# Gate projections as seven quarter products in a stage of their own, their sigmoids kept in DRAM

## The chip, the cores and the metric

The kernel runs on one core of a Trainium2 chip. The metric is the device time of one execution in microseconds (us). Before the change it is 2252.72 us, the median of three runs (2252.09 to 2253.51).

## What is computed

The reference is one decoder layer over 1024 tokens of width 1024, in float32. Three branches y_a (a linear recurrence), y_b (sliding-window attention) and y_c (dilated attention) read the same x. Each has a gate, and they are merged:

```python
proj = x @ w_in                      # gates: 3 x 1024 of its columns
...
ys = jnp.stack([y_a, y_b, y_c], axis=2)
branch = jnp.einsum('bsnc,ncd->bsnd', ys, w_branch)
merged = jnp.sum(jax.nn.sigmoid(gates.reshape(bsz, S, N_BRANCHES, D)) * branch, axis=2)
return merged @ w_out
```

A layer norm, a SwiGLU feed-forward part of width 2816 and a second layer norm follow.

## The kernel before

Activations lie transposed, channels on the 128 partitions and tokens along the free axis. Every float32 matrix product is made of three float32r products: an operand is split into `hi` (a cast on ScalarE, ACT) and `lo` (a subtraction on VectorE, DVE), and hi*hi, hi*lo and lo*hi are added in PSUM. So one 128-column chunk of a weight (8 k tiles of 128 x 128) against one half of the tokens (512) is 24 matmuls of 128x512.

The stages in order of time: projections and recurrence of branch a (to about 190 us), attention of y_b (to 440), attention of y_c (to 944), the gate and branch stage (944 to 1466), the output projection with the first layer norm (to 1599), the first feed-forward product (to 2002), the second with the last norm.

`WeightStream` (lines 44 to 126) feeds the weights. Each source is a chunk of 512 KB, loaded on SP's queue into a ring of two `w_raw` tiles, then split into `w_hi` and `w_lo` (rings of two). A step of the stream is a generator that issues matmuls and yields.

The gate and branch stage (lines 775 to 850 and 902 to 911) is a list `seq` of 48 jobs: three gate jobs, then a branch job and a gate job in turn. A gate job multiplies one chunk of the gate columns of `w_in` with `xh`/`xl`, the split x that has stayed in SBUF since the start; `gate_evac` writes the sigmoid into a ring of three `sg` tiles. A branch job does the same with a chunk of `w_branch` and with `yh`/`yl`, the split output of one branch, which `load_y` reads back from DRAM (`y_dram`). `branch_evac` multiplies by the sigmoid and adds to `merged`.

The first feed-forward product (lines 1054 to 1200) is done by seven products of quarters, Winograd's form of Strassen's scheme. The operand x is cut into four quarters, two halves of k by two halves of the tokens, and so are two weight chunks of 128 columns. Seven products (`a00`, `a01`, `s1` to `s4`, `a11`) of 12 matmuls each, 84 in a pair, stand for the eight (96 matmuls) of the plain way. POOL makes four sums `t` of weight quarters per pair, ACT and DVE split five half chunks (`ph`, `pl`) and, in all but the first four pairs, one whole chunk; DVE adds the banks in SBUF tiles `e`. In the first four pairs ("front" pairs) the products `a00` and `a01` have been done earlier, since their x quarters are ready first.

The order of instructions on each engine is not the order of the code alone: the scheduler of the framework reorders what has no dependence between it.

Of the kernel before, what the change touches and what calls it, by code (L numbers as in the profile page):

```python
# [148 lines left out]
def trunk_kernel(ctx: ExitStack, tc: tile.TileContext, x, x_t, w_in, conv_w, conv_b, w_rg, b_rg, w_ig, b_ig,  # L149
# [17 lines left out]
    x1_dram = dram.tile([KT, P, D], F32, name="x1_dram")  # L167
    g_dram = dram.tile([2, HT, P, HALF], F32, name="g_dram")
# [592 lines left out]

    drain(W.run(lead))
# [8 lines left out]
    va.close()  # L771
# [3 lines left out]
    a3 = ExitStack()  # L775
    acc8 = mk_pool(ctx, "acc8", bufs=8, space=PSUM)
    mg1 = mk_pool(a3, "mg1")
    mg3 = mk_pool(a3, "mg3", bufs=3)
    mg4 = mk_pool(a3, "mg4", bufs=4)
    merged = mg1.tile([P, KT, S], F32, name="merged")  # L780
    order = (1, 2, 0)
    LEAD = 3
    NB = 3 * KT
    sg = {}
    yparts = {}

    def load_y(n, hf):
        yh = mg1.tile([P, KT, HALF], F32R, tag=f"yh{hf}", name="yh")
        yl = mg1.tile([P, KT, HALF], F32R, tag=f"yl{hf}", name="yl")
        for k in range(KT):  # L790
            t = mg4.tile([P, HALF], F32, tag="yraw", name="yraw")
            act.dma_start(t, y_dram[n][k, :, hf * HALF:(hf + 1) * HALF])
            act.copy(yh[:, k, :], t)
            dve.tensor_sub(yl[:, k, :], t, yh[:, k, :].bitcast(F32))
        yparts[n, hf] = yh, yl

    def gate_evac(i):
        def f(hf, acc):
            if hf == 0:
                sg[i] = mg3.tile([P, S], F32, tag="sg", name="sg")  # L800
            act.activation(sg[i][:, hf * HALF:(hf + 1) * HALF], acc, AF.Sigmoid)
        return f
# [3 lines left out]
    def branch_evac(i):  # L806
        bi, dt = divmod(i, KT)

        def f(hf, acc):
            sl = slice(hf * HALF, (hf + 1) * HALF)  # L810
            m = merged[:, dt, sl]
            if bi == 0:
                dve.tensor_mul(m, sg[i][:, sl], acc)
                return
            t = sg[i][:, sl]
            dve.tensor_mul(t, t, acc)
            dve.tensor_add(m, m, t)
            first = NB - LEAD
            if i >= first:
                if i == first:  # L820
                    fin_h[hf] = xpool.tile([P, KT, HALF], F32R, tag=f"xh{hf}", name="mh")
                    fin_l[hf] = xpool.tile([P, KT, HALF], F32R, tag=f"xl{hf}", name="ml")
                for d in range(0 if i == first else dt, dt + 1):
                    m = merged[:, d, sl]
                    act.copy(fin_h[hf][:, d, :], m)
                    dve.tensor_sub(fin_l[hf][:, d, :], m, fin_h[hf][:, d, :].bitcast(F32))
        return f

    def gate_job(i):
        bi, dt = divmod(i, KT)  # L830
        proj_job(acc8, w_cols(w_in, C_G + order[bi] * D + dt * P), x_mov, gate_evac(i))

    def branch_job(i):
        bi, dt = divmod(i, KT)
        n = order[bi]

        def movs(hf, k):
            yh, yl = yparts[n, hf]
            return yh[:, k, :], yl[:, k, :]
        proj_job(acc8, w_cols(w_branch[n], dt * P), movs, branch_evac(i))  # L840

    seq = [("g", i) for i in range(LEAD)]
    for i in range(NB):
        seq.append(("b", i))
        if i + LEAD < NB:
            seq.append(("g", i + LEAD))
    ends = []
    for kind, i in seq:
        (gate_job if kind == "g" else branch_job)(i)
        ends.append(len(W.steps))  # L850
# [50 lines left out]

    load_y(order[0], 0)
    load_y(order[0], 1)
    for (kind, i), end in zip(seq, ends):
        last_of_branch = kind == "b" and i % KT == KT - 1 and i // KT < 2
        for j, c in enumerate(W.run(end)):
            if last_of_branch and j == 4:
                load_y(order[i // KT + 1], 0)
        if last_of_branch:
            load_y(order[i // KT + 1], 1)  # L910
    a3.close()

# [67 lines left out]

# [73 lines left out]
    def product(bank, op, bh, bl, start):  # L1054

        ah, al = ops[op]
        for k in range(4):
            wh, wl = bh[:, k * P:(k + 1) * P], bl[:, k * P:(k + 1) * P]
            mm(bank, wh, ah[:, k, :], start and k == 0, False)
            mm(bank, wh, al[:, k, :], False, False)  # L1060
            mm(bank, wl, ah[:, k, :], False, k == 3)
            if k % 2:
                yield 1296

    NA = 4
    front = {}

    def front_evac(bank, q):

        if q == 0:  # L1070
            t = frp.tile([P, HALF], F32, tag="p1", bufs=NA, name="p1")
            act.copy(t, bank)
        else:
            t = frp.tile([P, HALF], F32, tag="silu", bufs=NA, name="silu")
            act.activation(t, bank, AF.Silu)
        return t

    def front_step(j):

        def f(hi, lo):  # L1080
            bank = acc8.tile([P, HALF], F32, tag="acc", name="acc")
            got = []
            for q in range(2):
                sl = slice(q * HALF, (q + 1) * HALF)
                yield from product(bank, L_OPS[q], hi[:, sl], lo[:, sl], q == 0)
                got.append(front_evac(bank, q))
            front[j] = got
        W.add([w_cols(w_ffn_in, j * P)], [(0, f)])

    for j in range(NA):  # L1090
        front_step(j)
# [9 lines left out]
    sring = mk_pool(srS, "sring", side="right")  # L1101
    raws, parts = {}, {}

    def load_pair(j):
        raws[j] = []
        for c in (j * P, FF + j * P):
            t = stage.tile([P, 1024], F32, tag="w_raw", name="w_raw")
            sync.dma_start(t.rearrange("p (a b) -> p a b", b=P), w_cols(w_ffn_in, c))
            raws[j].append(t)

    def wsum(j, n, a, b, op):
        t = sring.tile([P, HALF], F32, tag="t", bufs=3, name="t")
        pool.tensor_tensor(t, a, b, op=op)  # L1113
        raws[j, n] = t

    def wsplit(j, n, src, width=HALF):
        if width == HALF:
            hi = sring.tile([P, HALF], F32R, tag="ph", bufs=7, name="ph")
            lo = sring.tile([P, HALF], F32R, tag="pl", bufs=7, name="pl")
        else:  # L1120
            hi = stage.tile([P, 1024], F32R, tag="w_hi", name="w_hi")
            lo = stage.tile([P, 1024], F32R, tag="w_lo", name="w_lo")
        act.copy(hi, src)  # L1123
        dve.tensor_sub(lo, src, hi.bitcast(F32))  # L1124
        parts[j, n] = hi, lo

    def prep(j):


        def b(k, c):  # L1130
            return raws[j][c][:, k * HALF:(k + 1) * HALF]

        def p1():
            wsum(j, "t1", b(0, 1), b(0, 0), OP.subtract)
            wsum(j, "t2", b(1, 1), raws[j, "t1"], OP.subtract)

        def p2():
            if j not in front:
                wsplit(j, "b0", raws[j][0], D)

        def p5():
            wsum(j, "t3", b(1, 1), b(0, 1), OP.subtract)
            wsplit(j, "t3", raws[j, "t3"])

        def p6():
            wsplit(j, "b11", b(1, 1))
            wsum(j, "t4", b(1, 0), raws[j, "t2"], OP.subtract)
            wsplit(j, "t4", raws[j, "t4"])
        return [lambda: load_pair(j), p1, p2, lambda: wsplit(j, "t2", raws[j, "t2"]),
                lambda: wsplit(j, "t1", raws[j, "t1"]), p5, p6]  # L1150

    def temp():
        return sring.tile([P, HALF], F32, tag="e", bufs=6, name="e")
# [3 lines left out]

    def pair(j, between):


        if j in front:
            between(0)
            p1, silu = front.pop(j)
        else:
            b0h, b0l = parts.pop((j, "b0"))
            ba = bank_()
            between(0)
            yield from product(ba, "a00", b0h[:, :HALF], b0l[:, :HALF], True)
            p1 = front_evac(ba, 0)
        between(1)  # L1170
        bb = bank_()
        yield from product(bb, "s2", *parts.pop((j, "t2")), True)
        u2 = temp()
        dve.tensor_add(u2, p1, bb)
        between(2)
        bc = bank_()
        yield from product(bc, "s1", *parts.pop((j, "t1")), True)
        v = temp()
        dve.tensor_add(v, u2, bc)
        between(3)  # L1180
        bd = bank_()
        yield from product(bd, "s3", *parts.pop((j, "t3")), True)
        dve.tensor_add(v, v, bd)
        between(4)
# [156 lines left out]
```

## Time and profile before

| | |
|---|---|
| profiled execution | 2260.57 us, of which 2258.8 us span |
| median of the three timed runs | 2252.72 us |
| TensorE (PE) busy | 98% of the span |
| VectorE (DVE), ScalarE (ACT), GpSimd (POOL) busy | 59%, 41%, 19% |
| granted TensorE clock, mean | 0.992 |
| DMA, mean over the span | 89 GB/s |

The span is from the first to the last instruction. A busy PE is not a PE at its peak: matmuls overlap, and each is shown longer than the distance to the next one. What a stretch costs is read from the starts: a row of the chain of waits that says "us, PE ..., xN" gives the distance of matmuls as us divided by N.

### The profile page before, as it was taken

The page shows a single profiled execution, that of the slowest core. Times are in us where ns is not written, and L with a number is a line of the kernel's source. Part 1 is how long each engine was busy: PE and PEld are TensorE (multiplying, and loading weights), DVE is VectorE, ACT ScalarE, POOL GpSimd, SP SyncE. Part 2 cuts the span into 40 slices and gives each one's busy share as a digit, 9 for nine tenths or more (in the row PEclk, how much of TensorE's full clock was granted, in tenths as well). Part 3 has the DMA queues.
Part 4 walks back from the last instruction along what each step waited for, and adds up shares of the span by engine and source line. Part 5 has one row for each costly group of instructions (what it writes and reads, how often), then busy time and mean ns, then how long its engine had stood idle before and what let it go on. Part 6 is the DMA issues. An engine that isn't in the chain of part 4 may idle for free.

```text
span 2258.8 us, 29437 instructions
## 1 busy us (share of the span) xinstructions
PE 2205.9 (98%) x11161; PEld 1870.4 (83%) x11161; DVE 1341.0 (59%) x2554; ACT 924.2 (41%) x1748; POOL 440.1 (19%) x411
## 2 busy tenths in 40 slices
PE   8999999999999999999999999999899999999998
PEld 6787888988899888888888888888778888888786
DVE  7888888776867768721142242459665445453735
ACT  4765776655655655521131131223233333342321
POOL 2332222212221222100000000002344334400301
PEclk9999999999999999999999999999999999999999
DMA  5123123112222223331131131154232222254543
GB/s 150 47 80 96 47 66 78 49 48 64 49 57 55 57 68 107 113 98 47 47 121 51 52 103 47 47 166 151 79 108 84 84 84 84 82 194 149 184 154 114
DMA packets 200654, 201.19 MB, mean 89 GB/s; under 512 B 9600, under 2 KB 156096, under 8 KB 200512
## 3 DMA queue, kind: packets, MB, share of 16 engines
q1 hardware_dynamic: 171232, 126.89, 18.7%
q0 software_dynamic: 14880, 45.14, 7.0%
q10 hardware_dynamic: 14400, 27.27, 3.8%
q8 instruction: 88, 1.44, 0.3%
q14 instruction: 54, 0.44, 0.1%
HBM read 152.08 MB, written 36.70 MB: 84 GB/s over the span
## 4 chain that ended last, share of the span: by engine, by line
PE 83%; DVE 9%; DMA 3%; issue 2%; ACT 2%; POOL 1%; SPq 0%; DVEq 0%; POOLq 0%; ACTq 0%
PE acc L185 71%; PE o L185 4%; PE s L185 4%; PE pt L542 4%; DVE xc L385 1%; DVE w_lo L97 1%; DMA w_raw<-in_w_ffn_in_dram 1%; DMA xin<-in_x_t_dram 1%; DVE pl L1124 1%; DMA x_dram<-r 1%; DVE r L964 1%; DVE r L961 1%; DMA res<-in_x_dram 1%; POOL t L1113 0%; DVE xc L382 0%
## 5 line engine op out<-in xcount | busy, mean ns | idle before, releaser
L185 PE MATMUL acc<-xh,w_hi 128*128 128x512 f32 x1056 | 418.7, 397 | 13.0 <-ACT w_hi L96 7.1
L185 PE MATMUL acc<-xl,w_hi 128*128 128x512 f32 x1056 | 415.8, 394 | 0.0
L185 PE MATMUL acc<-xh,w_lo 128*128 128x512 f32 x1056 | 415.4, 393 | 0.0
L96 ACT CAST w_hi<-w_raw 128x1024 fp32r<-128x1024 f32 x149 | 156.7, 1052 | 432.5 <-PE acc L185 390.1
L97 DVE TENSOR_TENSOR w_lo<-w_raw,w_hi 128x1024 fp32r<-128x1024 f32 x111 | 140.7, 1268 | 288.1 <-ACT w_hi L96 288.0
L185 PEld LDWEIGHTS acc<-xh,w_hi 128*128 128x128 f32 x1056 | 199.5, 189 | 52.4 <-ACT w_hi L96 7.1
L185 PEld LDWEIGHTS acc<-xh,w_lo 128*128 128x128 f32 x1056 | 199.4, 189 | 39.7 <-DVE w_lo L97 0.8
L185 PEld LDWEIGHTS acc<-xl,w_hi 128*128 128x128 f32 x1056 | 199.7, 189 | 37.4
L965 POOL TENSOR_TENSOR r<-r,ln_b 128x1024 f32<-128x1024 f32 x13 | 38.6, 2976 | 695.7 <-DMA res<-in_x_dram 572.8
L546 ACT CAST pt_h<-pt 128x512 fp32r<-128x512 f32 (+3 forms) x256 | 124.8, 500 | 92.3 <-PE pt L542 87.5
L547 DVE TENSOR_TENSOR pt_l<-pt,pt_h 128x512 fp32r<-128x512 f32 (+3 forms) x256 | 144.3, 572 | 20.7 <-ACT pt_h L546 18.3
L185 PE MATMUL acc<-yh,w_hi 128*128 128x512 f32 x384 | 149.4, 389 | 0.0
L185 PE MATMUL acc<-yl,w_hi 128*128 128x512 f32 x384 | 149.4, 389 | 0.0
L185 PE MATMUL acc<-yh,w_lo 128*128 128x512 f32 x384 | 149.4, 389 | 0.0
L537 POOL DMA_DIRECT2D y_dram<-yp x96 | 52.1, 543 | 425.2 <-DVE yp L536 326.2
L542 PE MATMUL pt<-ident,p 128*128 128x128 f32 x816 | 129.9, 278 | 1.6 <-DVE pt_l L547 0.8
L185 PE MATMUL o<-pt_h,v 128*128 128x256 f32 (+1 forms) x464 | 117.4, 275 | 1.8 <-DVE yp L536 1.8
L1123 ACT CAST ph<-t 128x512 fp32r<-128x512 f32 x88 | 53.9, 622 | 154.8 <-PE acc L185 82.1
L185 PE MATMUL acc<-w_lo,gh 128*128 128x512 f32 x288 | 113.2, 393 | 4.0 <-DVE w_lo L97 4.0
L185 PE MATMUL o<-pt_l,v 128*128 128x256 f32 (+1 forms) x464 | 113.9, 286 | 2.1 <-DVE pt_l L547 2.1
L629 ACT ACTIVATE p<-p,small 128x128 f32<-128x128 f32 (+7 forms) x128 | 99.5, 778 | 37.4 <-DVE small L626 36.0
L185 PE MATMUL acc<-w_hi,gl 128*128 128x512 f32 x288 | 112.9, 392 | 0.0
(330 smaller groups left out, 5071.9 us busy)
## 6 DMA issues: line engine op xcount, KB each, us to landing
w_raw<-in_w_in_dram SPq DMA_DIRECT2D x76, 512.0 KB, 3.8
w_raw<-in_w_ffn_in_dram SPq DMA_DIRECT2D x48, 512.0 KB, 4.5
w_raw<-in_w_ffn_out_dram SPq DMA_DIRECT2D x47, 512.0 KB, 3.7
w_raw<-in_w_branch_dram SPq DMA_DIRECT2D x24, 512.0 KB, 3.9
yraw<-y_dram ACTq DMA_DIRECT2D x48, 256.0 KB, 3.4
g_dram<-e POOLq DMA_DIRECT2D x44, 256.0 KB, 3.0
w_raw<-in_w_out_dram SPq DMA_DIRECT2D x12, 512.0 KB, 3.7
gl<-g_dram SPq DMA_DIRECT2D x22, 256.0 KB, 4.2
```

The source lines that it names most:

```text
L96: self.nc.scalar.copy(hi, raw)
L97: self.lo_engine.tensor_sub(lo, raw, hi.bitcast(F32))
L185: pe.matmul(o, a, b, start=start, stop=stop, skip_group_check=True)
L385: dve.scalar_tensor_tensor(xc, xr[:, 1 + j:1 + j + S], vec[:, j * 8 + ct:j * 8 + ct + 1], xc, op0=OP.mult, op1=OP.add)
L537: pool.dma_start(dst, yp[:, :n])
L542: pe.transpose(pt[:, i * P:(i + 1) * P], b, ident)
L546: act.copy(dst_h, v)
L547: dve.tensor_sub(dst_l, v, dst_h.bitcast(F32))
L629: act.activation(p[:, :n], p[:, :n], AF.Exp, bias=m, scale=-1.0, accum_out=sm[:, 1:2])
L961: dve.tensor_scalar(r[:, sl], r[:, sl], mv[:, 0:1], sm[:, 3:4], op0=OP.subtract, op1=OP.mult)
L965: adder.tensor_add(r[:, sl], r[:, sl], lnp["b"][:, sl])
L1123: act.copy(hi, src)
```

## The change

The sigmoids of all gates are computed in a stage ahead of the branch products, by the seven-product scheme, and written to a new DRAM buffer `sg_dram`; the branch stage reads them back, one 512 KB tile for each job. The code of the feed-forward pairs becomes a class `Pairs` that both stages use. For the feed-forward part its order differs in this: the last step of a pair's preparation (`b11` and `t4`) is made in the pair itself instead of in the one before, the next pair's load is issued two products later, `t4` is made in place of `t2` (two `t` tiles instead of three), and one sum is made in place of `u2`.

The x quarters for the sums are loaded again from the transposed input `x_t` (`load_xq`), two of the four k tiles on SP's queue in the last part of the attention and two on ACT's queue behind it; POOL and DVE make the sums (`x_sums`), ACT and DVE split them (`x_split`).

```diff
+    def load_xq(k, where, queue):
+        t = where.tile([P, 4, HALF], F32, tag="v", name="xq")
+        for q in range(4):
+            r, c = (q % 2 * 4 + k) * P, q // 2 * HALF
+            queue.dma_start(t[:, q, :], x_t[r:r + P, c:c + HALF])
+        xq[k] = [t[:, q, :] for q in range(4)]
+    def x_sums(k, eng):
+        a00, a01, a10, a11 = xq[k]
+        eng.tensor_add(a11, a10, a11)
+        eng.tensor_sub(a10, a00, a10)
+        eng.tensor_sub(a00, a11, a00)
+        pool.tensor_sub(a01, a01, a00)
...
+        if units is todo[-1][0]:
+            for k in range(2):
+                load_xq(k, vpool, sync)
+            for k in range(2):
+                x_sums(k, pool)
...
+        def pair(self, j, between):
...
+            between(1)
+            bb = self.bank()
+            yield from product(bb, "s2", *parts.pop((j, "t2")), True)
+            u2 = temp()
+            dve.tensor_add(u2, p1, bb)
+            between(2)
+            bc = self.bank()
+            yield from product(bc, "s1", *parts.pop((j, "t1")), True)
+            v = temp()
+            dve.tensor_add(v, u2, bc)
+            between(3)
+            bd = self.bank()
+            yield from product(bd, "s3", *parts.pop((j, "t3")), True)
+            dve.tensor_add(v, v, bd)
+            self.c11(j, v)
+            between(4)
+            if j >= self.na:
+                yield from product(ba, "a01", b0h[:, HALF:], b0l[:, HALF:], False)
+                self.c00(j, ba)
+            between(5)
+            yield from product(bc, "s4", *parts.pop((j, "b11")), False)
...
+            between(6)
+            yield from product(bd, "a11", *parts.pop((j, "t4")), False)
+            dve.tensor_add(u2, u2, bd)
+            self.c10(j, u2)
...
+                def between(i):
+                    if i == 1:
+                        cur[6]()
+                    elif nxt:
+                        for f in {2: nxt[:1], 4: nxt[1:3], 5: nxt[3:4], 6: nxt[4:6]}.get(i, ()):
+                            f()
...
+    NG = 3
...
+    def sig_out(j, tile_, half_, src, dst):
+        act.activation(dst, src, AF.Sigmoid)
+        act.dma_start(sg_dram[2 * j + tile_, :, half_ * HALF:(half_ + 1) * HALF], dst)
...
+    def x_split(k):
+        a00, a01, a10, a11 = xq[k]
+        for n, src in (("s2", a00), ("s1", a11), ("s3", a10), ("s4", a01)):
+            h, l = [o[:, k, :] for o in xops[n]]
+            act.copy(h, src)
+            dve.tensor_sub(l, src, h.bitcast(F32))
+    load_xq(2, vpool, act)
+    load_xq(3, yx, act)
+    for j in range(NG):
+        gate.front_step(j, j == 2)
...
+    def load_sg(i):
+        if i < NB:
+            sg[i] = mg3.tile([P, S], F32, tag="sg", name="sg")
+            pool.dma_start(sg[i], sg_dram[i])
-    def gate_job(i):
-        bi, dt = divmod(i, KT)
-        proj_job(acc8, w_cols(w_in, C_G + order[bi] * D + dt * P), x_mov, gate_evac(i))
...
+    gate.run(12, at, first, 2)
...
+    load_y(order[0], 1)
+    for n_, end in enumerate(ends):
+        for _ in W.run(end):
+            pass
+        if n_ % 7 == 1 and n_ < 14:
+            load_y(order[n_ // 7 + 1], 0)
+        if n_ == 2:
+            load_y(order[1], 1)
+        if n_ == 13:
+            load_y(order[2], 1)
```

Before, PE goes from the third gate chunk (`xh`, `xl` with `w_hi`, `w_lo`) to the first branch chunk (`yh`, `yl`), and on in turn:

```order
L185 MATMUL acc<-xh_93,w_hi 128x512
L185 MATMUL acc<-xl_95,w_hi 128x512
L185 MATMUL acc<-xh_93,w_lo 128x512
L185 MATMUL acc<-yh,w_hi 128x512
L185 MATMUL acc<-yl,w_hi 128x512
L185 MATMUL acc<-yh,w_lo 128x512
```

Now PE goes from the last front product (x quarter `xh_93` with half-chunk splits `ph`, `pl`) to the first pair's products, which read the split sums `gs2` (and `s1`, in the place of `xh_94`):

```order
L186 MATMUL acc<-xh_93,pl 128x512
L186 MATMUL acc<-gs2h,ph 128x512
L186 MATMUL acc<-gs2l,ph 128x512
L186 MATMUL acc<-xh_94,ph 128x512
L186 MATMUL acc<-xl_96,ph 128x512
L186 MATMUL acc<-gs2h,pl 128x512
```

72 front matmuls stand where the 144 of the three gate chunks stood first, and the pair's products come ahead of all branch work.

On DVE, the same place before: behind the last attention output (`yp`) come the `lo` parts of the first y (`yl`) and of the weights:

```order
L536 TENSOR_TENSOR yp<-o,yp 64x256
L794 TENSOR_TENSOR yl<-yraw,yh 128x512 x8
L97 TENSOR_TENSOR w_lo<-w_raw,w_hi 128x1024
L794 TENSOR_TENSOR yl<-yraw,yh 128x512 x8
L97 TENSOR_TENSOR w_lo<-w_raw,w_hi 128x1024 x2
```

And now, at the same place (the end of this stretch; `xq` are sums of x quarters, `gs2l` to `gs4l` and `xl_96` splits of them, `yv` the first y, `pl` splits of weight sums, `e` the first sum out of PSUM):

```order
L778 TENSOR_TENSOR xq<-xq 128x512
L1031 TENSOR_TENSOR yv<-yv 128x512 x2
L875 TENSOR_TENSOR pl<-t,ph 128x512 x2
L1031 TENSOR_TENSOR yv<-yv 128x512
L992 TENSOR_TENSOR gs3l<-xq,gs3h 128x512
L1031 TENSOR_TENSOR yv<-yv 128x512
L992 TENSOR_TENSOR gs2l<-xq,gs2h 128x512
L992 TENSOR_TENSOR gs4l<-xq,gs4h 128x512
L875 TENSOR_TENSOR pl<-t,ph 128x512
L875 TENSOR_TENSOR pl<-w_raw,ph 128x512
L875 TENSOR_TENSOR pl<-t,ph 128x512
L923 TENSOR_TENSOR e<-p_10225,acc 128x512
```

Between `yp` and that first `e` there are 31 DVE instructions of 128x512 now: 6 sums, 14 splits of sums, 4 of y, 2 of the third front chunk and 5 of the first pair's weights.

At the end of the gate stage, ACT issues the loads of the second half of the first y (`y_dram_58`) and of both halves of the second (`y_dram_59`) in one piece, mixed with the last sigmoids:

```order
L1029 DMA yl<-y_dram_58 128x512
L96 CAST w_hi<-w_raw 128x1024
L979 DMA sg_dram<-e 128x512
L1030 CAST yh<-yl 128x512
L1029 DMA yl<-y_dram_59 128x512
L1030 CAST yh<-yl 128x512
L1029 DMA yl<-y_dram_59 128x512
L978 ACTIVATE e<-e 128x512
```

Before, those loads were spread over two changes of branch.

## Rows read from the trace of the kernel before

**Rows 1.** Page, part 1: PE's busy time, share of the span, instructions.

```profile
PE 2205.9 (98%) x11161; PEld 1870.4 (83%) x11161; DVE 1341.0 (59%) x2554; ACT 924.2 (41%) x1748; POOL 440.1 (19%) x411
```

**Rows 2.** Windows: stretch and us; engines' busy us (count); PEclk, DMA share, GB/s.

```profile
944.20:1466.50 522.30, 522.30 (x2305) 432.60 (x2305) 150.67 (x189) 113.69 (x161) 0.53 (x1) 1.00 0.24 72
1560.00:1598.80 38.80, 33.52 (x174) 28.53 (x172) 33.27 (x48) 19.18 (x35) 4.53 (x3) 0.91 0.28 89
1598.80:1656.90 58.10, 55.27 (x230) 43.42 (x230) 37.08 (x49) 15.91 (x27) 26.37 (x23) 0.97 0.32 98
1656.90:2004.00 347.10, 347.10 (x1531) 287.53 (x1532) 178.23 (x246) 109.32 (x169) 129.26 (x106) 1.00 0.29 93
```

**Rows 3.** Chain of waits, whole span: start us, us, what was waited for.

```profile
944.20 561.55 PE acc L185 x2477
...
1656.89 454.32 PE acc L185 x2003
```

**Rows 4.** Groups by line, gate and branch stage: busy us, mean ns, idle before.

```profile
L185 PE MATMUL acc<-xh,w_hi 128*128 128x512 f32 x384 | 149.4, 389 | 0.0
...
L794 DVE TENSOR_TENSOR yl<-yraw,yh 128x512 fp32r<-128x512 f32 x48 | 31.9, 689 | 26.3 <-ACT yh L793 26.1
L793 ACT CAST yh<-yraw 128x512 fp32r<-128x512 f32 x48 | 28.9, 620 | 34.9 <-DMA yraw<-y_dram 19.9 <-PE acc L185 8.2 <-issue 4.1
L801 ACT ACTIVATE sg<-acc 128x512 f32<-128x512 f32 x48 | 28.4, 592 | 90.4 <-PE acc L185 88.0 <-DVE yl L794 1.9 <-issue 0.5
```

**Rows 5.** Groups by line, full pairs of the feed-forward stage.

```profile
L1124 DVE TENSOR_TENSOR pl<-t,ph 128x512 fp32r<-128x512 f32 x69 | 55.5, 804 | 15.7 <-ACT ph L1123 15.7
...
L1113 POOL TENSOR_TENSOR t<-w_raw 128x512 f32<-128x512 f32 x34 | 44.1, 1297 | 149.3 <-DMA w_raw<-in_w_ffn_in_dram 149.3
...
L1124 DVE TENSOR_TENSOR w_lo<-w_raw,w_hi 128x1024 fp32r<-128x1024 f32 x17 | 22.6, 1329 | 39.1 <-ACT w_hi L1123 39.1
...
L1179 DVE TENSOR_TENSOR e<-e,acc 128x512 f32<-128x512 f32 x18 | 12.4, 686 | 20.7 <-PE acc L185 20.7
```

**Rows 6.** Timeline of ACT from 944 us: start, us, instruction, idle before.

```profile
944.24 4.37 ACTq L792 DMA_DIRECT2D yraw<-y_dram  x4
948.71 0.62 ACT L793 CAST yh<-yraw 128x512 fp32r<-128x512 f32 x1 [4.11 <-issue]
950.07 0.62 ACT L793 CAST yh<-yraw 128x512 fp32r<-128x512 f32 x1 [0.74 <-DMA yraw<-y_dram]
950.13 0.33 ACTq L792 DMA_DIRECT2D yraw<-y_dram  x1
950.98 0.62 ACT L793 CAST yh<-yraw 128x512 fp32r<-128x512 f32 x1 [0.28 <-DMA yraw<-y_dram]
```

**Rows 7.** Timeline around 1614 us, POOL and DVE side by side.

```profile
1614.02 1.62 POOL L1113 TENSOR_TENSOR t<-w_raw,t 128x512 f32<-128x512 f32 x1 [1.29 <-DVE pl L1124]
1614.40 1.78 DVE L1124 TENSOR_TENSOR pl<-w_raw,ph 128x512 fp32r<-128x512 f32 x1
```

**Rows 8.** Waits of PE, 1560 to 2004 us: total us, times, longest.

```profile
PE acc L185 <- ACT ph L1123: 2.5, 3, 1.6
PE acc L185 <- DVE e L1179: 1.8, 2, 1.1
```

**Rows 9.** Chain of waits through the front pairs of the feed-forward stage.

```profile
1603.39 5.26 DMA w_raw<-in_w_ffn_in_dram
...
1608.82 1.30 POOL t L1113
...
1610.18 1.30 POOL t L1113
...
1612.16 1.28 DVE pl L1124 x2
...
1616.72 4.78 DMA w_raw<-in_w_ffn_in_dram
```

**Rows 10.** DMA issues: count, KB each, median us to landing.

```profile
yraw<-y_dram ACTq DMA_DIRECT2D x48, 256.0 KB, 3.4
```

More of the change, by code (lines that the diff above doesn't have):

```diff
@@ new lines, in trunk_kernel @@
+    load_xq(2, vpool, act)
+    load_xq(3, yx, act)
+    for j in range(NG):
+        gate.front_step(j, j == 2)
+    first = gate.prep(0)
+    for i, _ in enumerate(W.run()):
+        if i == 0:
+            gate.own_front(2)
+        if i % 2 == 0 and 2 <= i <= 8:
+            k = i // 2 - 1
+            if k >= 2:
+                x_sums(k, dve)
+            x_split(k)
+        if i == 8:
+            first[0]()
+            first[1]()
+    place = {(1, 0): 0, (1, 1): 1, (2, 0): 2, (2, 1): 3, (0, 0): 0, (0, 1): 3}
@@ L783, in trunk_kernel @@
     NB = 3 * KT
+    AHEAD = 3
+    yq = []
     sg = {}
@@ L900, in trunk_kernel @@
                             [wo_dest(k) for k in range(n)]))
[L902 to L910, printed above, removed]
     a3.close()
+    va.close()
     ff1 = mk_pool(ctx, "ff1")
@@ L1052, in trunk_kernel, with ffn_c00, ffn_c11, ffn_c01 @@
     later.extend(op_transposes((0, 1)))
[L1054 to L1063, printed above, removed]
-    NA = 4
[L1066 to L1088, printed above, removed]
+    NA = 4
+    silu = {}
+    sringp = []
+    def ffn_c00(j, bank):
+        t = frp.tile([P, HALF], F32, tag="silu", bufs=NA, name="silu")
+        act.activation(t, bank, AF.Silu)
+        silu[j] = t
+    def ffn_c11(j, v):
+        silu[j, 1] = v
+    def ffn_c01(j, g):
+        dve.tensor_mul(g, g, silu.pop(j))
+        pool.dma_start(g_dram[0, j], g)
+    def ffn_c10(j, g):
+        act.activation(g, g, AF.Silu)
+        dve.tensor_mul(g, g, silu.pop((j, 1)))
+        pool.dma_start(g_dram[1, j], g)
+    ffn = Pairs(lambda j: [w_cols(w_ffn_in, c) for c in (j * P, FF + j * P)], ops, sringp, [frp], NA,
+                ffn_c00, ffn_c01, ffn_c10, ffn_c11)
     for j in range(NA):
-        front_step(j)
+        ffn.front_step(j)
     run_steps(W.run(), 2)
@@ L1100, in trunk_kernel @@
     srS = ExitStack()
[L1101 to L1150, printed above, removed]
@@ L1152, in temp @@
[L1152 to L1153 removed]
+    sringp.append(mk_pool(srS, "sring", side="right"))
     def bank_():
         return acc8.tile([P, HALF], F32, tag="acc", name="acc")
[L1158 to L1184, printed above, removed]
[L1185 to L1200 removed]
@@ L1280, in ffn_done @@
             later.extend(rest)
-    for f in prep(0):
-        f()
-    for j in range(HT):
-        nxt = prep(j + 1) if j + 1 < HT else []
-        drain(pair(j, lambda n: nxt[n]() if nxt else None))
+    ffn.run(HT)
     srS.close()
```

228 lines of the change are left out of this document (170 added, 58 removed).

## The prediction

> **What bounds the kernel now.** I read part 1 of the page first: PE is busy for 98% of the span, and no other engine reaches 60% [rows 1]. That is an average, so the second view is the windows by stage. In the gate and branch stage PE is busy for all of 522.30 us at the full granted clock, while DVE, ACT and POOL work 150.67, 113.69 and 0.53 us [rows 2]. The groups of this stage say the same from the other side: PE waited 0.0 us before its matmuls, and ACT's sigmoids spent 88.0 us waiting for PE [rows 4]. Third, the chain of waits gives the price of a matmul. From 944.20 it is one piece, 561.55 us for 2477 matmuls, 0.2267 us each; the feed-forward part gives 454.32/2003 = 0.2268 us [rows 3]. So this stage is matmuls end to end, and its time is their number times 0.2268 us, as long as the other engines keep ahead. Fourth, the feed-forward stage shows what the new scheme does here. Its full pairs, 1656.9 to 2004, have PE busy for 347.10 of 347.10 us, but its beginning does not: 55.27 of 58.10 us in the front pairs and 33.52 of 38.80 us just before, with clocks of 0.97 and 0.91 [rows 2].
>
> **Removed: matmuls.** Before, 24 gate chunks of 48 matmuls (24 for each half of the tokens) are 1152. Now 12 pairs of 84 are 1008. 144 x 0.2268 = -32.7 us. The branch products keep their 1152. All of it lies on the bounding engine, so it counts in full.
>
> **Added: the start of the gate stage, +4.5 us.** PE's first work is the front products, 72 matmuls whose x quarters have stayed split in SBUF; then s2 and s1 of the first pair (12 each). s2 needs a split sum of all four k tiles, s3 another. From 944.2 PE has 96 x 0.2268 = 21.8 us of work if s2 is in time, so s3 is wanted at 966.0. Two of the four k tiles come only by loads that ACT issues behind the attention. Four such loads stand at this very place before: issued from 944.24, their casts start at 948.71 to 950.98 [rows 6], so I let the x quarters of k = 2 be there at 950.5. Behind them DVE has a fixed list, shown under the change: 29 instructions of 128x512 up to the lo part of t3's split. At 0.689 us [rows 4] that is 20.0 us, which ends at 970.5, 4.5 us late. ACT has fewer (its casts take 0.62 us [rows 6]) and does not set the end. What stands behind DVE's list in its queue are the evacuations, with 8 PSUM banks as slack.
>
> **The same start with POOL beside DVE: +2.** POOL makes two x sums and t1, t2, t3, t4 of the first pair in this stretch, 6 x 1.297 us [rows 5] = 7.8 us. One row pair shows the two engines side by side: a POOL sum took 1.62 us and a DVE split, begun during it, 1.78 us in place of 0.69 [rows 7], so 1.1 us was lost in that meeting. Over many, the mean is lighter: DVE's pl takes 0.804 us in the full pairs, where POOL's sums run too, against 0.689 without them [rows 4, 5]; 69 x 0.115 = 7.9 us, over 17 pairs of four sums 0.12 us a sum. So 6 sums cost between 0.7 and 7.8 us. I take 2, nearer the mean than the single meeting, since DVE's list is dense here and so meets more.
> The Trainium skill, "SBUF — State Buffer", section "SBUF: two separate sides", calls the pair of ports that DVE and GpSimd share an exclusive lock: the loser blocks for the whole instruction. It names DVE instructions with two SBUF inputs among the takers, and all of DVE's list are such. The 1.78 us row agrees with it and the 0.804 us mean shows that most instructions don't meet. By the rule at its hardest this term would be 7.8 and the sum 5.8 us later; that is the second rival below.
>
> **The first pairs behind it: +1, and the clock: +1.** The first three pairs have no a00 and a01 of their own, 60 matmuls or 13.6 us. Their weight chain (two chunks landing, two POOL sums, DVE splits, the next load) took 13.33 us from load to load in the feed-forward front pairs [rows 9], so there is nearly no slack. PE's waits from 1560 to 2004 were 2.5 us for ph and 1.8 us for e [rows 8], in four pairs and their start; I take 1 for three pairs, bounds 0 and 4.3. A PE that waits is also followed by a lower clock in this trace: 0.97 over 58.10 us is 1.7 us, 0.91 over the 38.80 us before it 3.5 us, most of which had PE waiting [rows 2]. I take 1, bounds 0 and 3.5.
>
> **Moved: the end of the attention, +0.5.** SP loads the first two k tiles of the x quarters there (8 loads of 256 KB), and POOL makes their 8 sums (8 x 1.297 = 10.4 us). ACT gets two casts more (2 x 0.62) and DVE two splits (2 x 0.69) in front of the first front product's weights. None of it is waited for by the attention itself; if DVE is held by each sum for as long as in the row pair (8 x 1.1), or SP's queue is late by one landing (3.4 us [rows 10]), up to 9 us of other engines' time are at stake, of which I let at most 3 reach PE.
>
> **The full pairs: 0.** Nine pairs of 84 x 0.2268 = 19.05 us. In one, DVE has 5 splits of halves and one whole (5 x 0.804 + 1.329) and 5 sums out of PSUM (5 x 0.686), 8.8 us [rows 5]; POOL four sums, 5.2 us; ACT the casts of the same (5 x 0.62 + 1.24), four sigmoids of 0.592, a copy of 0.6, and four issues of 0.33, 8.6 us [rows 4, 6]. All are under half of PE's time. The load-to-load chain of 13.33 us [rows 9] fits too. The feed-forward pairs, which add a load from DRAM and multiplications, ran without a gap [rows 2]. If that cover went, the price would be that of the fourth rival.
>
> **The change to the branch products: 0.** ACT now issues 24 loads of y in one piece, each with its cast: 24 x (0.33 + 0.62) = 22.8 us. The weights of the third branch chunk are cast behind 19 of them and some sigmoids, 19 x 0.95 + 6 x 0.62 = 21.8 us; they begin some 5.4 us before the last gate product ends, so the cast is due out 16.4 us behind it. PE has two chunks, 96 x 0.2268 = 21.8 us, before it wants it. 5.4 us of slack, so 0; if each load waits for its landing (3.4 us in place of 0.33 for some of them), +6. The read-back of sg adds 12.6 MB written and 12.6 MB read, (25.2 MB)/(490 us) = 51 GB/s to 72 [rows 2]; the full pairs ran at 93 without a wait. The multiplies wait for sg instead of for nothing; three tiles are loaded ahead and a chunk of PE takes 10.9 us against a landing of 3.4 us for 256 KB [rows 10].
>
> **The feed-forward pairs in their new order: 0.** Its front pairs lost 4.3 us [rows 8]. Loading later and making t4 in the pair itself can cost that once more, or save it: bounds -3.4 and +3.4. The full pairs have the slack worked out above.
>
> **Sum.** -32.7 + 4.5 + 2 + 1 + 1 + 0.5 = -23.7 us. The profiled execution took 2260.57 us, so one of the changed kernel would take 2236.9. The median of the timed runs is 7.85 us below the profiled execution; with the same difference the forecast is 2252.72 - 23.7 = 2229.0 us. Its own range, from terms that move by 1 to 4 us each, is 2224 to 2234.
>
> **Rivals.**
> 1. The start is covered (chance 0.16). DVE's list is shorter in effect, because the sums of k = 2 begin as soon as two quarters land, and PE arrives late itself from the attention's end. For it: the casts in [rows 6] start one by one with their loads. Against it: the list has no gaps to give back. Only 1 to 2 us of 9 are lost: 2252.72 - 32.7 + 1.5 = 2221.5 us.
> 2. DVE and POOL shut each other out at the start (0.18): the term is 7.8 in place of 2, 2252.72 - 23.7 + 5.8 = 2234.8 us. For it the 1.78 us row [rows 7], against it the 0.804 us mean [rows 5].
> 3. The one piece of y loads holds ACT (0.08): +6, 2235 us. For it: ACT's casts of y waited 19.9 us for landings before [rows 4]. Against it: they waited since they had nothing else to do.
> 4. Slower (0.04): the full gate pairs are paced not by PE but by the chain through the two raw chunks (load, t sums, splits, next load), with ACT's queue, which now also issues the sigmoids' writes, in it. A write issued by ACT has to wait for its sigmoid, and the cast behind it for both. The gain is gone when each of the nine full pairs takes 19.05 + 23.7/9 = 21.7 us. At 24 us they cost 9 x 4.95 = 45 us, and the time is 2229 + 45 = 2274 us. Against it: 13.33 us [rows 9], and the feed-forward stage's windows [rows 2].
> That the change doesn't do what it says is not a rival with a chance: PE's list of instructions is shorter by exactly these 144 matmuls.
>
> **Chances.** Forecast 0.54, the rivals as given. 2221 to 2239 holds the forecast, nearly all of rivals 1 to 3 and a second mishap of 4 us on the forecast; what is left out is the fourth and the tails, under 0.2. A change of under 0.2% (4.5 us) can't be told from none. All cases but the fourth lie more than 13 us below 2252.72; I leave 0.03 for a mixture that ends within 4.5 us, so faster is 0.93, slower 0.04.
>
> **What would show it.** In the windows of the changed kernel the gate and branch stages have PE busy throughout but for one hole, of 4 to 8 us, 16 to 25 us behind their start, where PE waits for DVE's gs3 or gs2 parts or for pl or ph (right for the start), and no hole near the first branch product (right for ACT's queue). The stage of 522 us is about 499 long. DVE's instructions there at 0.69 mean rival 1, many at 1.2 to 1.8 rival 2. A PE that waits in every full pair, or fewer than 0.95 busy between the front pairs and the first branch chunk, would make the forecast wrong, and so would a new wait ahead of 944 us.

## The result and the profile after

The changed kernel takes 2237.70 us (median of 5 runs, 2235.38 to 2241.35), the kernel before 2253.51 in the same series. The ratio is 0.9927, with a 95% interval of 0.9908 to 0.9946: about 16.5 us faster (12 to 21), where 23.7 were forecast. The time lies inside the range of 2221 to 2239, at its upper end, and outside the forecast's own range of 2224 to 2234.

The profiled execution took 2235.38 us. PE has the 144 matmuls less that it should have (part 1 of the page, as in [rows 1]):

```profile
PE 2173.8 (97%) x11017; PEld 1840.5 (82%) x11017; DVE 1421.0 (64%) x2685; ACT 962.7 (43%) x1825; POOL 539.8 (24%) x493
```

The windows, with the columns of [rows 2]. The first two are the gate stage (front products and start, then the rest), the next two the branch products, then output projection with norm, front pairs and full pairs of the feed-forward part:

```profile
943.20:990.00 46.80, 37.66 (x148) 29.05 (x147) 31.79 (x43) 24.56 (x44) 20.43 (x11) 0.93 0.51 166
990.00:1185.30 195.30, 195.30 (x863) 161.67 (x862) 85.42 (x119) 70.82 (x114) 52.63 (x40) 1.00 0.37 119
1185.30:1215.00 29.70, 26.31 (x108) 20.99 (x108) 19.52 (x29) 16.22 (x27) 2.67 (x5) 0.93 0.86 299
1215.00:1454.30 239.30, 238.37 (x1046) 196.97 (x1045) 96.42 (x130) 40.38 (x52) 10.06 (x20) 0.99 0.36 115
1454.30:1579.70 125.40, 121.99 (x594) 101.66 (x592) 92.85 (x128) 40.40 (x64) 19.71 (x8) 1.00 0.43 139
1579.70:1634.00 54.30, 52.97 (x229) 42.52 (x230) 31.97 (x47) 14.50 (x25) 25.82 (x23) 1.00 0.33 105
1634.00:1979.40 345.40, 345.40 (x1524) 285.88 (x1524) 176.13 (x245) 109.26 (x170) 134.22 (x106) 1.00 0.29 92
```

The full gate pairs are as dense as forecast. Both other pieces of the new stages are not: the start has PE busy for 37.66 of 46.80 us, the first branch chunks for 26.31 of 29.70, both at a clock of 0.93. By the starts of the matmuls, the gate stage takes 242.3 us for 1008 matmuls (228.6 at 0.2268) and the branch products 269.0 for 1152 (261.3). Together that is 511.3 us against 522.3 before, 11.0 less instead of 32.7: 13.7 us are lost in the start and 7.7 in the branch products. In the start the three holes are 5.1, 0.9 and 3.6 us, each start of a matmul to the next less 0.2268; behind the first and the third PE starts its matmuls 0.43 us apart for a while, the lower of its two clock levels (1.2 GHz), which costs 3.0; small delays of single matmuls make up the other 1.1.

PE's waits in the start, and then in the branch products (as [rows 8]):

```profile
PE acc L186 <- ACT p L831: 4.9, 1, 4.9
PE acc L186 <- ACT ph L874: 3.5, 1, 3.5
PE acc L186 <- DVE gs2l L992: 0.7, 1, 0.7
```

```profile
PE acc L186 <- ACT w_hi L96: 2.9, 2, 2.0
PE acc L186 <- DVE w_lo L97: 1.4, 1, 1.4
```

The chain of waits leads to what was late in each (start us, us, what; cut at the dots):

```profile
953.38 6.41 POOL xq L779
961.79 9.49 PE acc L186 x34
973.81 7.18 DMA w_raw<-in_w_in_dram
981.16 1.81 POOL t L864
985.00 195.08 PE acc L186 x852
...
1189.95 13.80 DMA w_raw<-in_w_branch_dram
1211.85 154.38 PE acc L186 x668
```

The first is a POOL sum of x quarters that takes 6.40 us in place of 1.3. Its neighbours in time, on POOL, DVE and ACT, one fence each (columns as [rows 6]):

```profile
953.38 6.40 POOL L779 TENSOR_TENSOR xq<-xq 128x512 f32<-128x512 f32 x1 [8.51 <-DVE xq L778]
```

```profile
953.16 0.68 DVE L992 TENSOR_TENSOR gs4l<-xq,gs4h 128x512 fp32r<-128x512 f32 x1
...
957.98 0.68 DVE L992 TENSOR_TENSOR gs2l<-xq,gs2h 128x512 fp32r<-128x512 f32 x1
960.46 1.09 DVE L992 TENSOR_TENSOR gs4l<-xq,gs4h 128x512 fp32r<-128x512 f32 x1 [1.80 <-ACT gs4h L991]
961.48 1.76 DVE L992 TENSOR_TENSOR xl<-xq,xh 128x512 fp32r<-128x512 f32 x1
```

```profile
955.32 0.60 ACT L978 ACTIVATE e<-acc 128x512 f32<-128x512 f32 x1
959.81 0.62 ACT L991 CAST gs4h<-xq 128x512 fp32r<-128x512 f32 x1 [3.89 <-POOL xq L779]
...
961.15 0.58 ACT L831 COPY p<-acc 128x512 f32<-128x512 f32 x1 [0.21 <-ACT xh L991]
```

DVE starts an instruction every 0.60 us (the dots stand for seven of them) and has no gap until 958.66; the sum ends 1.1 us behind that, so it ran in DVE's first gap. ACT's next cast needs this sum, and ACT takes its queue in order, so the copy of the third front product out of PSUM stands behind it. PE waits 4.9 us for that copy, though nothing that the copy needs is late.

### The profile page after: what moved, and what is told of

It is laid out like the page before. It is cut to its first block, busy times and chain, and to the rows that moved or that the text cites. A ratio compares the mean times of both kernels' runs of the same rounds, so it can differ in the third digit from the quotient of the medians.

```text
span 2233.6 us, 29700 instructions
## 1 busy us (share of the span) xinstructions
PE 2173.8 (97%) x11017; PEld 1840.5 (82%) x11017; DVE 1421.0 (64%) x2685; ACT 962.7 (43%) x1825; POOL 539.8 (24%) x493
## 4 chain that ended last, share of the span: by engine, by line
PE 80%; DVE 8%; issue 4%; DMA 4%; ACT 2%; POOL 1%; SPq 0%; ACTq 0%; DVEq 0%; POOLq 0%
PE acc L186 68%; PE o L186 4%; PE s L186 4%; PE pt L543 4%; DVE xc L386 1%; DVE w_lo L97 1%; POOL t L864 1%; DMA xin<-in_x_t_dram 1%; DMA w_raw<-in_w_branch_dram 1%; DMA yl<-y_dram 1%; DVE r L1217 0%; DVE xc L383 0%; DVE r L1214 0%; DMA w_raw<-in_w_ffn_in_dram 0%; DVE pt_l L548 0%
## 5 line engine op out<-in xcount | busy, mean ns | idle before, releaser
L186 PE MATMUL acc<-xh,w_hi 128*128 128x512 f32 x760 | 303.3, 399 | 12.9 <-ACT w_hi L96 7.8
L186 PE MATMUL acc<-xl,w_hi 128*128 128x512 f32 x760 | 300.5, 395 | 0.0
L186 PE MATMUL acc<-xh,w_lo 128*128 128x512 f32 x760 | 300.0, 395 | 0.0
L186 PEld LDWEIGHTS acc<-xh,w_hi 128*128 128x128 f32 x760 | 143.9, 189 | 40.9 <-ACT w_hi L96 7.8
L864 POOL TENSOR_TENSOR t<-w_raw 128x512 f32<-128x512 f32 x68 | 97.0, 1427 | 312.0 <-DMA w_raw<-in_w_ffn_in_dram 194.1
L186 PEld LDWEIGHTS acc<-xh,w_lo 128*128 128x128 f32 x760 | 143.7, 189 | 28.3 <-DVE w_lo L97 0.8
L186 PEld LDWEIGHTS acc<-xl,w_hi 128*128 128x128 f32 x760 | 143.8, 189 | 25.7
L875 DVE TENSOR_TENSOR pl<-t,ph 128x512 fp32r<-128x512 f32 x136 | 102.9, 762 | 82.3 <-ACT ph L874 82.1
L97 POOL TENSOR_TENSOR w_lo<-w_raw,w_hi 128x1024 fp32r<-128x1024 f32 x38 | 91.4, 2406 | 97.5 <-ACT w_hi L96 91.4
L186 PE MATMUL s<-kh,q 128*128 128x256 f32 (+3 forms) x320 | 103.8, 333 | 1.0 <-DVE small L572 0.5
```

What stands on the lines that cost most here:

```text
L97: self.lo_engine.tensor_sub(lo, raw, hi.bitcast(F32))
L186: pe.matmul(o, a, b, start=start, stop=stop, skip_group_check=True)
```

## The experiments

Stage times below are by the starts of the matmuls. My theory after the result: (a) the hole at 957 is POOL shut out by DVE and passed on by ACT's queue; (b) the hole at 1207 comes from the piece of y loads; (c) the feed-forward pairs' new order saves 3.6 us. Rivals: DVE's list binds the start anyway, the weights' ring tile comes free late, and (c) is scatter. Of each edit only the lines that matter are shown.

**The a01 sums on DVE.**

```diff
-        pool.tensor_sub(a01, a01, a00)
+        eng.tensor_sub(a01, a01, a00)
```

> The a01 sums of the last two x quarters move from POOL to DVE. In the changed kernel the first of them takes 6.40 us on POOL, from 953.38, beside a DVE that has no gap until 958.66; ACT's next cast waits for it, and PE waits 4.9 us for ACT's copy. Theory (POOL is shut out by DVE, and ACT's queue passes that on): the 4.9 us wait goes, the front products run without a hole, and of the 9.6 us of holes between 943 and 990 about 4 go, although DVE's list is 1.4 us longer; the gate stage (first gate product behind the attention to the first branch product, 242.3 us) takes 237 to 239. Rival (DVE's list is the bound anyway, its last part of s2 is out at 972 in either case): the hole moves behind the front products, to the wait for gs2's lo part, and the stage keeps 241 to 244.

Measured: 2236.95 us, ratio 0.9918 (0.9902 to 0.9935), not to be told from the changed kernel. The gate stage keeps 241.2 us, as the rival had it. But the 4.9 us wait fell to 1.3, and a new one of 3.2 us, for ACT's `ph`, took its place: POOL's next instruction, the first weight sum, was shut out instead; it ends 1.1 us behind DVE's first gap, which begins at 962.45.

```profile
958.03 5.53 POOL L864 TENSOR_TENSOR t<-w_raw 128x512 f32<-128x512 f32 x1 [12.78 <-DMA w_raw<-in_w_in_dram]
```

So the cause named was right and the cure was not: whichever POOL sum comes first in DVE's gapless stretch pays.

The branch products are left alone by this edit, yet they take 266.1 us here in place of 269.0. The hole at 1207 is 1.8 us in place of 3.8, without a lower clock behind it, and PE waits there for the weight's `lo` alone:

```profile
PE acc L186 <- DVE w_lo L97: 1.5, 1, 1.5
```

A later run that leaves this place alone too, e6, shows the same: 265.7 us and 1.6 us for `w_lo`. So about 3 of the 7.7 us lost in the branch products of the changed kernel's profiled execution do not come with this order every time.

**The later y loads paced.** Each piece, but for the second half of the third y, is issued behind the cast of a weight chunk on ACT (`W.cast` is the latest such cast; `NO_SYNC` orders two instructions of one engine, without a wait).

```diff
-            act.dma_start(raw, y_dram[n][k, ...])
+            ld = act.dma_start(raw, y_dram[n][k, ...])
+            if pace:
+                tc.add_manual_dep(ld.ins, W.cast.ins.name, NO_SYNC, reason="paced")
```

> The y loads of the second and third branch are issued one piece at a time behind the casts of later weight chunks, not in one run. In the changed kernel PE waits 3.7 us at 1207 and the weight chunk that it waits for took 13.80 us to land; the branch products take 269.0 us for 1152 matmuls (261.3 at 0.2268). Theory (the piece of y loads delays the weights, by ACT's queue or by the DMA engines): no hole, clock 1.00, the branch products take 262 to 265 us. Rival (the weights come late since their ring tile came free late, whatever the y loads do): the hole stays, 268 to 270 us.

Measured: 2234.44 us, ratio 0.9902 (0.9881 to 0.9923), not to be told from the changed kernel; branch products 265.2 us. The hole at 1207 is gone, so the ring tile (the rival) was not what was late. Against e1 and e6 the edit takes away a hole of 1.8 us, not of 3.8. What remains is one wait for `w_hi`, at the change to the third branch, where the loads were not paced; it was there in the changed kernel too:

```profile
PE acc L186 <- ACT w_hi L96: 2.1, 1, 2.1
```

**Loads in one piece, casts late.**

```diff
-            act.copy(yh[k], raw)
+            cp = act.copy(yh[k], raw)
+            if pace:
+                tc.add_manual_dep(cp.ins, W.cast.ins.name, NO_SYNC, reason="paced")
```

> The y loads are issued in one piece as in the changed kernel, but their casts stand behind the casts of later weight chunks on ACT. Theory A (ACT's queue holds the weight cast: it stood 4.4 us behind the landing): the hole at the third branch chunk falls from 3.7 to under 1 us, though the load still lands late. Theory B (the DMA engines are crowded: 299 GB/s, landing after 13.80 us): the landing stays over 10 us and the hole stays at 2 us or more.

Measured, in a single execution: 2234.11 us, branch products 265.0 us, no hole at the third chunk. The DMA engines were as crowded as can be, and PE went on:

```profile
1184.30:1214.30 30.00, 30.00 (x134) 24.86 (x133) 17.50 (x26) 12.35 (x20) 2.71 (x5) 1.00 0.98 342
```

The weight chunk still took 11.7 us to land. Its cast ran 19.7 us behind the first branch product, and PE wants it at 21.8; in the changed kernel it ran at 22.8, 4.4 us behind the landing of its chunk, with y casts and y issues ahead of it:

```profile
1203.94 1.05 ACT L96 CAST w_hi<-w_raw 128x1024 fp32r<-128x1024 f32 x1 [9.63 <-DMA yl<-y_dram]
```

```profile
1208.18 1.04 ACT L96 CAST w_hi<-w_raw 128x1024 fp32r<-128x1024 f32 x1
```

So theory A holds against B: the crowd alone does not reach PE. But ACT's queue is not the whole of it. With its casts, the edit moves y's `lo` parts on DVE too, and in the changed kernel these and sums into `merged` stood ahead of the weight's `lo`, which PE wanted next:

```profile
1208.18 1.29 DVE L1031 TENSOR_TENSOR yl<-yl,yh 128x512 fp32r<-128x512 f32 x2
1209.38 1.28 DVE L1046 TENSOR_TENSOR merged<-sg,acc 128x512 f32<-128x512 f32 x2
1210.58 1.22 DVE L97 TENSOR_TENSOR w_lo<-w_raw,w_hi 128x1024 fp32r<-128x1024 f32 x1
```

By the starts of the matmuls 2.2 of the 3.8 us are the wait for `w_hi` and 1.6 the wait for `w_lo`. The part on DVE is the one that e1 and e6 have as well.

**The new order of the feed-forward pairs alone** (the kernel before with the class `Pairs` in that part, nothing else).

> The kernel before with the new order of the feed-forward pairs alone; gates and branches as before. First feed-forward product from its first pair to the first product of the second part: 403.4 us before, 399.8 in the changed kernel. Theory (the new order saves the waits of the front pairs): 399 to 401 us, the whole kernel 2 to 4 us faster than before. Rival (that difference and the 7 us between the end of the branch products and the first pair are scatter of single executions): 402 to 405 us and no difference in the timed runs.

Measured: 2255.39 us against 2255.76, ratio 0.9998 (0.9989 to 1.0007). The stage does take 399.9 us in the trace, but the timed runs show no gain, and the interval leaves none above 2.5 us. The second product took 247.9 us in place of 246.1; with the new gates it takes 244.3 to 249.9 in ten executions, so that says little.

**The kernel before, again.**

> The kernel before once more, for a second look at its stages. Theory (the execution profiled first was a long one): gates and branches 522.3 us again, but the first feed-forward product 400 to 402 us in place of 403.4, or output projection and norm 126 to 130 in place of 132.5, so that these stages' differences to the changed kernel are mostly scatter. Rival (they belong to the kernel before): 403 to 404 and 131 to 133 us.

Measured: 2255.46 us; gates and branches 522.3 again, first feed-forward product 403.4 again, output projection and norm 126.6. So the 403.4 belongs to the kernel before, and the 132.5 us of its first profile do not: this stage took 126.6 to 132.5 in three executions with the old gates and 125.0 to 129.8 in the ten with the new.

**The first y late.** Its loads stand behind a cast of the tenth pair, `gate.cast`.

```diff
-            load_y(order[0], 0)
+            load_y(order[0], 0, gate.cast)
```

> The loads of the first half of the first y, which the order drew into the start of the gate stage, stand behind a cast of the tenth pair. DVE's list at the start is 4 splits shorter, ACT's 4 casts and 8 issues. Theory: the 5 us hole stays (DVE's gapless stretch from 949 to 958.7 holds no y split), the later two, 0.9 and 3.6 us, lose about 2 together; gate stage 239 to 241.5 us in place of 242.3. Rival (the y loads crowd the DMA engines, and the second pair's weights, which took 7.18 us to land, come in 4): the 3.6 us hole goes too, 236 to 238.5 us.

Measured, in a single execution: 2231.21 us, gate stage 236.9. The rival was right: the two later holes are gone. All that is left is the first one, with its POOL sum 7.00 us long:

```profile
956.30 7.00 POOL L779 TENSOR_TENSOR xq<-xq 128x512 f32<-128x512 f32 x1 [10.37 <-DVE xq L778]
```

```profile
PE acc L186 <- ACT p L831: 6.0, 1, 6.0
```

The shorter lists and the freer DMA engines can both have done it, and for the 3.6 us hole the traces tell them apart. The load that the second pair waited for was issued 30.8 us behind the stage's start in the changed kernel (973.81) and 30.5 here, so the lists gave 0.3 us. It landed after 7.18 us there and 3.7 here, and POOL's sum came 3.9 us sooner:

```profile
974.57 0.37 SPq L859 DMA_DIRECT2D w_raw<-in_w_in_dram  x1
```

```profile
978.31 1.29 POOL L864 TENSOR_TENSOR t<-w_raw 128x512 f32<-128x512 f32 x1 [6.18 <-DMA w_raw<-in_w_in_dram]
```

What took away the 0.9 us hole, for `gs2l` on DVE, was not taken apart.

**All three edits** (sums on DVE, first y late, later casts late).

> All three edits: a01 sums on DVE, the first y late, the casts of later y behind the weights' casts at both changes of branch. Theory (each hole has the cause named for it): gate stage 236 to 238.5 us, branch products 262 to 263.5, and the kernel 10 to 13 us under the changed one, some 2225 us or 0.988 of before. Rival (POOL's next sum is shut out in place of the one taken away): the gate stage keeps 240 to 242 us and the kernel is at 2229 to 2233.

Measured: 2227.28 us, ratio 0.9872 (0.9855 to 0.9889); gate stage 236.2, branch products 263.5. Two holes in the start were left (1.1 and 3.3 us, the second behind a POOL sum of 6.12 us), and 2.2 us at 1360.

**A fourth front pair**, and four split tiles in place of five, for room (the last number).

```diff
-    NG = 3
+    NG = 4
...
-                 lambda j, v: sig_out(j, 1, 1, v, v), 4, 5)
+                 lambda j, v: sig_out(j, 1, 1, v, v), 4, 4)
```

> The last kernel with a fourth front pair (24 more matmuls ahead of the first pair that needs sums, 5.4 us of PE) and, to make room, four split tiles in place of five. Theory (the holes at the start are DVE's list being late, so work ahead of it hides them): 0 to 3 us of holes at the start, gate stage 230 to 234 us, kernel 2219 to 2224. Rival (four split tiles make the full pairs wait, or the fourth pair's two splits lengthen the list as much as they give): 236 us or more.

Measured: 2239.91 us, ratio 0.9923 (0.9909 to 0.9936), slower than without it; gate stage 246.3. The start has fewer holes, but the full pairs are no longer dense, 195.78 of 203.50 us behind 985. PE waits there for DVE's sums out of PSUM, which share DVE's queue with the splits:

```profile
PE acc L186 <- DVE e L932: 3.2, 3, 2.0
PE acc L186 <- DVE e L928: 2.8, 1, 2.8
```

The likely cause is that DVE's splits now wait for a free tile and hold the sums behind them; that is argued, not shown, since pair and tiles were changed together.

**The first pair's weight sums on DVE.**

```diff
-            pool.tensor_tensor(t, a, b, op=op)
+            (dve if self.own_sums and j == 0 else pool).tensor_tensor(t, a, b, op=op)
...
-                pool.tensor_sub(t, b(1, 0), t)
+                (dve if self.own_sums and j == 0 else pool).tensor_sub(t, b(1, 0), t)
```

> The e7 kernel with the four weight sums of the first gate pair on DVE, so that POOL has no sum in the start (its first there took 6.12 us in e7, beside a gapless DVE, and PE waited 3.3 us for the cast behind it). Theory (a POOL sum waits for a gap of DVE, so at this place PE pays its wait): the two holes of e7, 1.1 and 3.3 us, shrink to 1 to 2.5 together although DVE's list is 2.8 us longer, and no DVE instruction in the start takes over 0.7 us; gate stage 234 to 235.5 us in place of 236.2. Rival (the two engines take turns anyway, so it doesn't matter which of them makes the sums): holes of 4 to 6 us, gate stage 236 to 238.

Measured, in a single execution: 2225.73 us, gate stage 234.2. POOL does nothing from 944.4 to 972.4; DVE runs from 949.05 to 968.6 almost without a gap, each instruction at 0.69 us, and PE's waits in the start are 2.6 us together in place of 4.1:

```profile
972.41 1.28 POOL L865 TENSOR_TENSOR t<-w_raw 128x512 f32<-128x512 f32 x1 [28.06 <-DMA w_raw<-in_w_in_dram]
```

The list is longer and the stage shorter, so the exclusion was the cost, not the number of sums. The difference is small beside the scatter (the changed kernel's start gave stages of 240.6 to 243.5 us in three executions), but the next two runs keep this edit and have 233.8 and 234.0.

**The second half of the third y behind the weight cast.**

```diff
+            if n_ == 14 and q == 4:
+                load_y(order[2], 1, None, W.cast)
...
-        if n_ == 13:
-            load_y(order[2], 1, None, W.cast)
```

> e9 with the second half of the third y issued later in the program, its casts behind the weight cast that PE waited 2.2 us for at 1360 in e7 (there three y casts, each waiting for its load, stood ahead of it). Theory (ACT's queue is the cause): that hole goes, branch products 261.3 to 262 us in place of 263.5; kernel 2221 to 2226. Rival (the y parts themselves come too late then): PE waits for yl or yh at the next half, branch products 263 or more.

Measured: 2223.56 us, ratio 0.9864 (0.9848 to 0.9879). The hole is gone and the branch products are matmuls end to end, at their price:

```profile
1178.70:1439.80 261.10, 261.10 (x1153) 216.15 (x1152) 115.51 (x159) 56.05 (x79) 12.73 (x24) 1.00 0.44 140
```

**What is wanted last, last.** The s4 parts of x behind the second weight sum on DVE.

> e10 with the parts of the first pair that are wanted last (the a01 sums and s4 splits of x) behind the second weight sum on DVE, 6 instructions or 3.6 us of its list. Theory (DVE's list up to s2 sets the first hole): holes at the start under 1.5 us, gate stage 230.5 to 234 us. Rival (the landing of the first pair's weights at 957 and of the last x quarter sets it): no difference to e10, 234 to 236 us.

Measured: 2222.06 us, ratio 0.9856 (0.9839 to 0.9873), not to be told from e10; gate stage 234.0. One hole of 2.3 us is left at the same place. The rival had the time right, but its cause does not follow: in e10 PE waited for ACT's `ph` of the first pair, now it waits for DVE's `pl`.

```profile
PE acc L186 <- DVE pl L881: 2.2, 1, 2.2
```

DVE's rows say why (cut at the dots). The edit brought the second sum forward to 960.44, but the parts put behind it still stand ahead of the sum's own split:

```profile
960.44 0.68 DVE L867 TENSOR_TENSOR t<-w_raw,t 128x512 f32<-128x512 f32 x1
961.04 1.28 DVE L998 TENSOR_TENSOR gs4l<-xq,gs4h 128x512 fp32r<-128x512 f32 x2
962.25 0.68 DVE L780 TENSOR_TENSOR xq<-xq 128x512 f32<-128x512 f32 x1
...
964.65 1.28 DVE L881 TENSOR_TENSOR pl<-t,ph 128x512 fp32r<-128x512 f32 x2
```

So the list that PE waits for became no shorter, and whether it or a landing sets this last hole was not tested. This version and e10 beat both kernels, by 30 to 32 us and 14 to 16 us.

## Why the prediction was right and where it was wrong

**Right:** the 144 matmuls and their price. e10 shows it whole: branch products at 0.2267 us each, full gate pairs dense, 494.9 us for both stages, 27.4 less than before. The 5.3 us that are missing to 32.7 are what is left of the start. Right too that the full pairs are covered. The start does lose time, but not as the forecast had it, in one hole 16 to 25 us behind the stage's start: there are three, 13, 28 and 38 us behind it, and the first and longest is for ACT's copy, which was not among the tiles named.

**Wrong, the step "the same start with POOL beside DVE: +2".** The size was between the bounds of 0.7 and 7.8, but I asked what POOL's sums do to DVE. It was DVE that did it to POOL: one sum waited 5.1 us for a gap. And I put the price on DVE's list, where PE would meet it at s2 or s3; it came by ACT's queue, to a front product that I had counted as covered. The mean of 0.804 us misled: it is over stretches in which DVE has gaps (178.23 of 347.10 us busy, [rows 2]), and DVE had none from 949 to 958.66. That is the second rival's mechanism, which I gave 0.18.

The kernel before could have told it. [rows 7] shows a meeting in which DVE waits, but half of POOL's sums in the full pairs take 1.944 us, not the 1.297 that I put down for all of them; one is shown beside the DVE instruction that it waits for:

```profile
L1113 POOL TENSOR_TENSOR t<-w_raw,t 128x512 f32<-128x512 f32 x34 | 66.1, 1944 | 9.8 <-DVE pl L1124 8.4
```

```profile
1712.26 1.42 DVE L1124 TENSOR_TENSOR w_lo<-w_raw,w_hi 128x1024 fp32r<-128x1024 f32 x1 [2.29 <-ACT w_hi L1123]
1712.67 2.16 POOL L1113 TENSOR_TENSOR t<-w_raw,t 128x512 f32<-128x512 f32 x1
```

The sum ends 1.15 us behind the split, as the long one of the start ends 1.12 us behind DVE's first gap.

The Trainium skill ("SBUF — State Buffer", "SBUF: two separate sides") says that the shared ports are an exclusive lock, held for the whole instruction, and that the other engine blocks. The row just shown agrees with it. The start goes further: POOL stayed out for nine DVE instructions, not for one.

**Mis-sized, the steps "the start: +4.5" and "the clock: +1".** DVE's list ended at 973.1, not 970.5, but PE, held until 961.8 by the copy, met it for only 0.9 us. The lower clock behind the holes cost 3.0 us, near its upper bound of 3.5.

**Wrong, the step "the first pairs behind it: +1".** It was 3.6 us, near the upper bound of 4.3. e6 shows why: the order drew eight loads of the first y into the start, with their casts and splits. I had counted four splits on DVE, but not the loads' share of the DMA engines, beside which the second pair's weights took 7.18 us to land in place of 3.7. All in all the start cost 13.7 us (5.1 + 0.9 + 3.6 + 3.0 + 1.1) where the terms gave 8.5 without the attention's.

**Wrong, the step "the change to the branch products: 0".** I worked out 16.4 us for ACT's list and 5.4 us of slack, by issues of 0.33 us and casts of 0.62, as if nothing in the list waited. In the trace a y cast waits for its load, the loads take 5.7 us instead of 3.4, and the weight cast stands behind them: it ran 22.8 us behind the last gate product, not 16.4.

```profile
yl<-y_dram ACTq DMA_DIRECT2D x32, 256.0 KB, 5.7
```

I also left out that DVE's queue has the same list, y's `lo` parts ahead of the weight's. It cost 3.8 us of holes there, 2.7 by the lower clock behind them (until 1217.6), and 1.2 at the third branch, a place that I had not worked out; 7.7 in all. In e1 and e6, with the same order here, it cost 4.9 and 4.5. This is the third rival, to which I gave 0.08 and +6. Two rivals that I priced one by one came together.

**The feed-forward pairs, 0:** the first product does take 3.5 us less, but e4 shows no gain in the timed runs, so 0 fits the kernel; where the 3.5 us go is not shown.

**How the forecast still came within 9 us.** The two stages gained 11.0 us in the profiled execution, 13 less than the 24.2 forecast for them; the timed gain is only 7 us smaller. Part of the difference is that one execution: the means of three with the same start (the changed kernel, e2, e3: 242.1) and of three with the same branch stage (the changed kernel, e1, e6: 266.9) make 509.0 us, a gain of 13.3. The rest is luck, not foresight. In the profiled executions output projection and norm are 7.1 us shorter, which no term foresaw, and most of it is the scatter that e5 shows. On the mean of all executions this stage is 3.5 us shorter with the new gates (126.4 us of ten against 129.9 of three); three are too few to call that an effect, and it stays open.

## What to carry to other kernels

Price an in-order queue by what its head waits for, not by the sum of its durations: a cast whose load is late holds every cast behind it, needed or not, and the longest hole here and the one at 1207 came by that way. Where DVE has a gapless list, the first sum given to POOL was not beside it but behind it; here it paid to give that stretch's sums to DVE itself, though its list grew. When a scheduler may draw loads ahead, look in the order for what it pulls into the stretch with least slack.

## What the runs showed of the hardware

A POOL sum of two SBUF operands, 1.3 us alone, took 5.53 to 7.00 us in six kernels (the changed one, e1, e2, e3, e6, e7) and 3.37 in e8. It was each time POOL's first sum of the start, and it ended 1.12 to 1.14 us behind the first gap of DVE's run of two-operand instructions, which kept their 0.68 us. Where POOL had begun, DVE's next took 1.76 us. So in these stretches DVE kept POOL out for as long as its run lasted, not for one instruction.

That is not the whole rule. A little later in the changed kernel DVE shows no gap either, and POOL's sums got in behind a single DVE instruction each; DVE's next then waited for them:

```profile
966.82 1.67 POOL L901 TENSOR_TENSOR t<-w_raw,t 128x512 f32<-128x512 f32 x1 [1.23 <-DVE pl L875]
968.46 1.74 POOL L864 TENSOR_TENSOR t<-w_raw 128x512 f32<-128x512 f32 x1
```

```profile
966.06 1.28 DVE L875 TENSOR_TENSOR pl<-t,ph 128x512 fp32r<-128x512 f32 x2
967.26 1.78 DVE L1031 TENSOR_TENSOR yv<-yv 128x512 fp32r<-128x512 f32 x1
968.96 1.78 DVE L992 TENSOR_TENSOR gs3l<-xq,gs3h 128x512 fp32r<-128x512 f32 x1
```

What decides between the two no run here shows.

DMA engines at 0.98 busy and 342 GB/s did not slow PE in e3: the weights landed after 11.7 us, 16.8 us behind the first branch product, and were wanted at 21.8. In the start of the changed kernel a weight load that took 3.5 us longer to land than in e6 did reach PE, which waited 3.6 us.
